# Layer 0's output projection by Strassen's seven products of quarters, in a two-layer retention and attention backbone

## The chip, the cores and the metric

The kernel runs on one core of one Trainium2 chip. The metric is device microseconds for one launch. A core has TensorE (PE in the profile, with its weight loads as PEld), VectorE (DVE), ScalarE (ACT), GpSimd (POOL) and SyncE (SP). Each engine takes its own instructions strictly in order and waits on semaphores; here SP issues all loads, and ACT issues the stores.

## The reference, cut to what matters

Two layers, one of retention and one of windowed attention, are applied to 256 latent tokens; 256 context tokens go through layer 0 with them. The model width is 2048, layer 0 has 8 heads of 512 value features. What the change touches is the end of layer 0, for all 512 tokens:

```python
def finish(o, g):
    b, h, l, dv = o.shape
    on = o * lax.rsqrt(jnp.mean(o * o, axis=-1, keepdims=True) + EPS)
    on = on.transpose(0, 2, 1, 3).reshape(b, l, h * dv) * norm_gain.astype(jnp.float32)
    return (on.astype(g.dtype) * jax.nn.silu(g)) @ w_out
...
x = x + gt_l[:, None] * y_l
if with_ctx_out:
    ctx = ctx + gt_c * y_c
```

So the operand u (4096 features by 512 tokens) is the normalised retention output times a gate, and the output projection is a product of a 2048 x 4096 weight with u. Everything is float32.

## The kernel before, in words

**Precision.** A float32 matrix product is made of three matmuls in a rounded 32-bit format: each operand is split into a high part (ACT casts it, `split`, `split_w`) and a low part (DVE subtracts the high part from the operand, `sub`, line 112). `mm3` adds high times high, high times low and low times high into one PSUM bank, each matmul streaming 512 columns. The kernel has a second form in layer 1 (`gemm_ws2`, lines 166 to 205): high and low part of 256 tokens lie side by side, so that one matmul of 512 columns does high times (high, low), and one of 256 columns does low times high.

**Weights.** Each weight piece is a 512 KB tile of 128 x 1024 (`wraw`, three buffers), loaded by SP, cast by ACT (line 131, `wh`, three buffers) and subtracted on DVE (line 112, `wl`, three buffers). In the three-matmul form one piece feeds 24 matmuls.

**Layer 0.** A loop over 8 heads makes gates, queries and keys, scores, values and outputs. A queue of small tasks (scores, outputs, norms) is drawn from between weight pieces (`hook`, `pump`). Each head's gated output is multiplied by its norm and gain (`spill`) and stored to DRAM in `uT_d`, head by head, because the next head needs the space. While the heads run, DVE also computes the modulation vectors of both layers as dot products (line 632).

**The output projection before.** Four chunks of 512 output features; each takes all 16 pairs of feature blocks of u, 24 matmuls a pair. The first chunk loads and splits u (`u_load`) while head 7's last tasks run in it. The epilogue of a chunk multiplies by the gate vector, adds the residual x, stores the latent half and squares it for the next norm (`residual`, `square`). The last chunk's tail is split by token half, so that the next norm's scale is ready early. Then the attention layer's keys follow (`k_part`), with the modulation of x1 (`mod1`) between weight pieces.

**What sets the order.** A scheduler orders each engine's instructions when the kernel is built, from the order in which the code is written, the data and the buffers' release; on the chip the order is fixed.

## Time and profile before

| what | value |
| --- | --- |
| time, median of 3 runs | 1997.96 us (1997.8 to 1998.27) |
| the profiled execution's own time | 1997.04 us |
| its span, from first to last instruction | 1995.2 us |
| TensorE busy | 1971.2 us, 99% of the span |
| VectorE busy | 1189.7 us, 60% |
| ScalarE busy | 682.3 us, 34% |
| GpSimd busy | 259.2 us, 13%, 89 instructions |
| granted TensorE clock | 1.00 |

The rows of the profile name a line of the kernel, an engine, an operation, what it writes and reads, and the shape as partitions times elements. A matmul's duration in a row covers its whole passage, while matmuls follow each other faster than that; so the pace of TensorE is read from the starting times of a run of them. Idle time in a row belongs to the instruction's engine and is named with what ended it.

### The profile page before, as it was taken

What the parts mean: (1) busy time and instruction counts of PE and PEld (TensorE: products, weight loads), DVE (VectorE), ACT (ScalarE), POOL (GpSimd) and SP (SyncE); (2) the same over time, 40 slices, a digit from 0 to 9 for tenths busy, and PEclk for the clock granted to TensorE, in tenths of its full rate; (3) what the DMA queues carried; (4) which work ended last, traced back from release to release, by engine and by line L of the source; (5) the groups of instructions that cost most, each with busy time, mean ns of one, the idle gap of its engine ahead of it and who ended that gap; (6) DMA issues with size and microseconds to landing.
All of it is one profiled execution on the core that took longest, in us unless ns stands there. A gap on an engine that the chain in (4) does not pass through costs nothing.

```text
span 1995.2 us, 24873 instructions
## 1 busy us (share of the span) xinstructions
PE 1971.2 (99%) x9381; PEld 1626.1 (82%) x9381; DVE 1189.7 (60%) x2320; ACT 682.3 (34%) x1003; POOL 259.2 (13%) x89
## 2 busy tenths in 40 slices
PE   6999999999999999999999999999999999999999
PEld 3678888888888888888888888888888888888887
DVE  5566224778788787786565345433232755777764
ACT  4234223232232232232232234322122434766653
POOL 1217414104104004004000001000000010000001
PEclk9999999999999999999999999999999999999999
DMA  9962334656556555655554335733332234444455
GB/s 377 417 224 87 103 102 147 198 179 201 173 184 187 183 185 179 190 185 179 190 186 166 107 99 165 275 105 108 102 107 95 95 101 156 140 137 130 150 195 170
DMA packets 121080, 332.24 MB, mean 167 GB/s; under 512 B 12480, under 2 KB 27136, under 8 KB 116736
## 3 DMA queue, kind: packets, MB, share of 16 engines
q1 hardware_dynamic: 107312, 315.95, 47.9%
q10 hardware_dynamic: 13648, 14.72, 2.2%
q8 instruction: 73, 1.20, 0.2%
q14 instruction: 47, 0.39, 0.1%
HBM read 318.00 MB, written 12.62 MB: 166 GB/s over the span
## 4 chain that ended last, share of the span: by engine, by line
PE 95%; DMA 2%; DVE 1%; issue 1%; ACT 0%; SPq 0%; POOL 0%; POOLq 0%; DVEq 0%; ACTq 0%
PE acc L138 25%; PE acc L139 25%; PE acc L140 25%; PE acc L189 5%; PE acc L186 3%; PE pm L138 3%; PE pm L140 3%; PE pm L139 3%; PE acc L476 2%; DMA araw<-in_adaS 1%; PE pm L413 1%; PE pm L1048 1%; DMA rows<-gamT_d 1%; DMA xp<-in_xT 0%; PE pm L247 0%
## 5 line engine op out<-in xcount | busy, mean ns | idle before, releaser
L112 DVE TENSOR_TENSOR wl<-wraw,wh 128x1024 fp32r<-128x1024 f32 x368 | 450.0, 1225 | 579.6 <-ACT wh L131 577.9
L131 ACT CAST wh<-wraw 128x1024 fp32r<-128x1024 f32 x367 | 385.0, 1052 | 957.6 <-PE acc L139 582.5
L138 PE MATMUL acc<-hT_h,wh 128*128 128x512 f32 x1184 | 462.8, 391 | 0.6 <-DVE r_l L112 0.6
L139 PE MATMUL acc<-hl,wh 128*128 128x512 f32 x1184 | 461.1, 389 | 0.0
L140 PE MATMUL acc<-hT_h,wl 128*128 128x512 f32 x1184 | 460.7, 389 | 0.0
L632 DVE SCALAR_TENSOR_TENSOR ajunk<-abraw,crow 128x512 bf16<-128x512 f32 x448 | 320.1, 714 | 8.6
L140 PE MATMUL acc<-wh,hl 128*128 128x512 f32 x704 | 274.1, 390 | 0.0
L138 PEld LDWEIGHTS acc<-hT_h,wh 128*128 128x128 f32 x1184 | 222.4, 188 | 46.8 <-issue 1.3
L140 PEld LDWEIGHTS acc<-hT_h,wl 128*128 128x128 f32 x1184 | 222.3, 188 | 46.7
L139 PEld LDWEIGHTS acc<-hl,wh 128*128 128x128 f32 x1184 | 222.5, 188 | 44.3
L693 POOL TENSOR_TENSOR dd<-two,dd 128x128 f32<-128x128 f32 x8 | 167.9, 20995 | 486.4 <-DVE dd L691 486.4
L139 PE MATMUL acc<-wl,hT_h 128*128 128x512 f32 x576 | 224.4, 390 | 0.0
L138 PE MATMUL acc<-wh,hT_h 128*128 128x512 f32 x576 | 224.3, 389 | 0.0
L140 PEld LDWEIGHTS acc<-wh,hl 128*128 128x128 f32 x704 | 132.1, 188 | 28.1 <-DVE hl L273 0.7
L138 PEld LDWEIGHTS acc<-wh,hT_h 128*128 128x128 f32 x576 | 108.2, 188 | 22.2 <-issue 0.3
L139 PEld LDWEIGHTS acc<-wl,hT_h 128*128 128x128 f32 x576 | 108.2, 188 | 21.9
L239 POOL TENSOR_TENSOR rs<-ms,mhalf 128x4 f32<-128x4 f32 (+1 forms) x23 | 32.5, 1412 | 616.8 <-DVE ms L236 324.0
L743 POOL TENSOR_TENSOR ossq<-ossq,osq 128x512 f32<-128x512 f32 x24 | 31.3, 1306 | 414.5 <-ACT osq L740 414.5
L138 PE MATMUL acc<-wh,hl 128*128 128x512 f32 x192 | 75.5, 393 | 0.0
L139 PE MATMUL acc<-wl,hl 128*128 128x512 f32 x192 | 74.8, 390 | 0.0
L138 PE MATMUL pm<-r_h 128*128 128x512 f32 (+1 forms) x208 | 71.5, 344 | 0.0
L140 PE MATMUL pm<-r_h,r_l 128*128 128x512 f32 (+1 forms) x208 | 71.2, 342 | 0.0
(233 smaller groups left out, 2374.3 us busy)
## 6 DMA issues: line engine op xcount, KB each, us to landing
wraw<-in_w SPq DMA_DIRECT2D x272, 512.0 KB, 3.5
abraw<-in_adaB SPq DMA_DIRECT2D x256, 256.0 KB, 3.2
wraw<-in_wo SPq DMA_DIRECT2D x96, 512.0 KB, 3.5
araw<-in_adaS SPq DMA_DIRECT2D x28, 1024.0 KB, 13.0
uT_d<-ue ACTq DMA_DIRECT2D x32, 256.0 KB, 2.8
wraw<-uT_d SPq DMA_DIRECT2D x16, 512.0 KB, 4.2
araw<-in_adaS SPq DMA_DIRECT2D x8, 512.0 KB, 9.4
x<-in_xT SPq DMA_DIRECT2D x4, 1024.0 KB, 8.0
```

The source lines that it names most:

```text
L112: return nc.vector.tensor_tensor(out=out, in0=a, in1=hi.bitcast(F32), op=ALU.subtract)
L131: last_hi[0] = nc.scalar.copy(wh, raw).ins
L138: nc.tensor.matmul(ps, lhsT=ah, rhs=bh, start=start, stop=False, skip_group_check=skip)
L139: nc.tensor.matmul(ps, lhsT=ah, rhs=bl, start=False, stop=False, skip_group_check=skip)
L140: return nc.tensor.matmul(ps, lhsT=al, rhs=bh, start=False, stop=stop, skip_group_check=skip).ins
L186: nc.tensor.matmul(accs[j][:, 0:L], lhsT=wk, rhs=h1(kb, s)[:, 0], start=False, stop=(kb == 2 * nkp - 1))
L189: nc.tensor.matmul(accs[j], lhsT=wk, rhs=h1(kb, s).rearrange("p a t -> p (a t)"), start=(kb == 0), stop=False)
L239: nc.gpsimd.tensor_tensor(out=rs, in0=ms, in1=mhalf.to_broadcast([P, n]), op=ALU.pow)
L476: last = nc.tensor.matmul(qk0[j], lhsT=a_[:, kb % 2, j * P:(j + 1) * P], rhs=b_, start=(kb == 0 and p == 0), stop=(kb == KB - 1 and p == 2))
L632: nc.vector.scalar_tensor_tensor(out=junk, in0=raw, scalar=1.0, in1=crow[:, t, q * 512:(q + 1) * 512], op0=ALU.mult, op1=ALU.mult, accum_o ...
L693: nc.gpsimd.tensor_tensor(out=dd, in0=two.to_broadcast([P, P]), in1=dd, op=ALU.pow)
L743: nc.gpsimd.tensor_tensor(out=ssq, in0=ssq, in1=sq, op=ALU.add)
```

## The change

The product is computed by Strassen's scheme over quarters. The 4096 features of u are split in two halves (in each head the first and the last two blocks of 128), the tokens in latent and context, the output features in two halves of 1024. Seven products M1 to M7, each of a 1024 x 2048 weight combination with a 2048 x 256 operand combination, replace eight.

- **Operands.** `parts` makes the five sums and differences of u's quarters that five products need, and stores them with the two plain quarters in `uB_d`; on GpSimd for heads 0 to 6, and for head 7 on DVE where the first two products need them. `prep` loads such a piece, and `split` makes its high and low part, side by side.
- **Weights.** `quarter` loads one 512 KB tile of a quarter of the weight, `comb` adds or subtracts two of them on GpSimd (128 x 1024), and `split_w` follows as before. M4 and M3 take a plain quarter, the other five a combination. The tiles come from a ring of seven buffers (three as before, four that held the low part of the layer's input).
- **Matmuls.** `piece` is the second form above: 8 matmuls of 512 columns and 8 of 256 for one weight tile. Four rounds r of 256 output features, in each four steps kq, and two products at a time: stage 1 is M4 with M1, stage 2 M5 with M7, stage 3 M2 with M6, stage 4 M3 alone.
- **Epilogue.** `done1` to `done4` add and subtract the products into x1 (ACT copies one half of a bank, DVE adds the other, GpSimd joins products with `comb`); `residual` now loads x piece by piece. The latent half is complete after stage 3, so its modulation runs under stage 4 (`hook4`).
- **Last head.** Head 7's gate product moves to the end of the layer, with the output tasks and the first operand loads between its weight pieces; its gating comes after it.

The host's layout of the weight changes to match. In the middle of the projection the engines' orders differ as follows.

**GpSimd, in the program before, from the end of the heads on.** The rows are the running sum of squares of a head's outputs (`ossq`), a reciprocal root (`rs`), the two reciprocal roots behind the projection (128x2), and then at once the attention layer's tables.

```order
L743 TENSOR_TENSOR ossq_9675<-ossq_9675,osq_9740 128x512
L743 TENSOR_TENSOR ossq_9675<-ossq_9675,osq_9793 128x512
L743 TENSOR_TENSOR ossq_9675<-ossq_9675,osq_9846 128x512
L239 TENSOR_TENSOR rs_9893<-ms_9891,mhalf_86 128x4
L239 TENSOR_TENSOR rs_11867<-ms_11864,mhalf_86 128x2
L239 TENSOR_TENSOR rs_11942<-ms_11939,mhalf_86 128x2
...
L949 TENSOR_TENSOR ktab_12298<-ropeA_12293,vec_72 128x128
```

Between the fourth and the fifth of these rows GpSimd had nothing to do for the whole projection.

**GpSimd, in the change, around the second round of stage 3.** `wraw` are tiles of the weight ring, combined by `comb` (line 911); `tmp` is M2 on its way into x1.

```order
L911 TENSOR_TENSOR wraw_11846<-wraw_11844,wraw_11846 128x1024
L911 TENSOR_TENSOR wraw_11848<-wraw_11844,wraw_11848 128x1024
L911 TENSOR_TENSOR x1_9874<-x1_9874,tmp_9877 128x2x256
L911 TENSOR_TENSOR wraw_11894<-wraw_11892,wraw_11894 128x1024
L911 TENSOR_TENSOR wraw_11896<-wraw_11892,wraw_11896 128x1024
L911 TENSOR_TENSOR wraw_11948<-wraw_11946,wraw_11948 128x1024
L911 TENSOR_TENSOR wraw_11950<-wraw_11946,wraw_11950 128x1024
L911 TENSOR_TENSOR wraw_12010<-wraw_12008,wraw_12010 128x1024
L911 TENSOR_TENSOR wraw_12012<-wraw_12008,wraw_12012 128x1024
L911 TENSOR_TENSOR wraw_12072<-wraw_12070,wraw_12072 128x1024
L911 TENSOR_TENSOR x1_9874<-x1_9874,tmp_9877 128x2x256
```

Now every weight tile of stages 2 and 3 passes through GpSimd first, two a step, and the join of a finished product stands between them in the same queue.

**VectorE, in the program before, at the end of a chunk.** `wl` is the low part of a weight piece, L846 the residual out of PSUM (`acc`), L859 the sum of squares.

```order
L112 TENSOR_TENSOR wl<-wraw,wh 128x1024 x15
L846 SCALAR_TENSOR_TENSOR x_10312<-acc,gt_91,x_10312 128x256 x4
L859 TENSOR_TENSOR ssq_10313<-ssq_10313,pm 128x512
L846 SCALAR_TENSOR_TENSOR x_10312<-acc,gt_91,x_10312 128x256
L859 TENSOR_TENSOR ssq_10313<-ssq_10313,pm 128x512
L846 SCALAR_TENSOR_TENSOR x_10312<-acc,gt_91,x_10312 128x256 x3
L112 TENSOR_TENSOR wl<-wraw,wh 128x1024
L859 TENSOR_TENSOR ssq_10313<-ssq_10313,pm 128x512 x2
```

Sixteen subtractions to a chunk, with the epilogue after them.

**VectorE, in the change, at the end of a round of stage 3.** L937 adds the two halves of M2's banks, L1032 subtracts M2 from x1, L941 adds M6 out of its banks, L960 is the residual out of a loaded x tile.

```order
L960 SCALAR_TENSOR_TENSOR x1_9874<-x1_9874,gt0_91,wraw_12220 128x256 x2
L112 TENSOR_TENSOR wl_12242<-wraw_12236,wh_12241 128x1024
L112 TENSOR_TENSOR wl_12269<-wraw_12238,wh_12268 128x1024
L937 TENSOR_TENSOR tmp_9877<-acc_12066,tmp_9877 128x256
L937 TENSOR_TENSOR tmp_9877<-acc_12067,tmp_9877 128x256
L1032 TENSOR_TENSOR x1_9874<-x1_9874,tmp_9877 128x2x256
L112 TENSOR_TENSOR wl_12304<-wraw_12298,wh_12303 128x1024
L941 TENSOR_TENSOR x1_9874<-acc_12068,x1_9874 128x256
L941 TENSOR_TENSOR x1_9874<-acc_12069,x1_9874 128x256
...
L112 TENSOR_TENSOR wl_12325<-wraw_12300,wh_12324 128x1024
```

Eight subtractions to a round, 28 rounds of a product instead of four chunks, and an epilogue between them that also waits for the round's matmuls.

```diff
+    uB_d = dram.tile([7, H, P, 2, L], F32, name="uB_d")
...
+    home = {M4: R_[0:8], M1: R_[8:10] + T_[0:5] + H_[7:8], M5: h_, M7: H_[5:7] + R_[2:8],
+            M2: R_[0:2] + R_[8:10] + T_[0:4], M6: T_[4:5] + H_[7:8] + R_[2:8], M3: h_}
...
+    ring, ring_n = [None] * 3, [0]
+
+    def raw_tile():
+        i = ring[ring_n[0] % len(ring)]
...
+    def prep(m, us):
+
+        raw = raw_tile().rearrange("p h (f t) -> p h f t", f=2)
+        nc.sync.dma_start(out=raw[:, :len(us)], in_=uB_d[m, us[0]:us[-1] + 1].rearrange("h p f t -> p h f t"))
+        for i, u in enumerate(us):
+            b = unit(m, u)
+            split(b[:, :, 0:L], b[:, :, L:T], raw[:, i])
...
+            if gated:
+                nc.vector.tensor_tensor(out=sg[:, f, :], in0=op, in1=sg[:, f, :], op=ALU.mult)
+            else:
+                nc.scalar.copy(sg[:, f, :], op)
...
+        def parts(h, u, to=None):
+
+            a, b, c, d = (u[:, 2 * k:2 * k + 2, L * t:L * t + L] for k in range(2) for t in range(2))
+            for m, x, y, op in ((M4, a, c, ALU.subtract), (M1, a, d, ALU.add), (M6, a, b, ALU.add),
+                                (M7, c, d, ALU.add), (M3, b, d, ALU.subtract)):
+                ue = pb.tile([P, 2, L], F32, name="ue", tag="ue", bufs=2)
+                now = to is not None and m in (M1, M4)
+                (nc.vector if now else nc.gpsimd).tensor_tensor(out=ue, in0=x, in1=y, op=op)
+                if now:
+                    split(to[m][:, :, 0:L], to[m][:, :, L:T], ue)
+                else:
+                    nc.scalar.dma_start(out=uB_d[m, h], in_=ue)
+            for m, x in ((M2, a), (M5, d)):
+                nc.scalar.dma_start(out=uB_d[m, h], in_=x)
...
+        sg = pb.tile([P, 4, 512], F32, name="sg", tag="sg")
+        output_tasks(H - 1, sg, gated=False)
+        for i, u in zip((1, 2, 4, 5, 7), range(2, 7)):
+            tasks.insert(i, lambda u=u: prep(M1, [u]))
+        for u in range(7):
+            tasks.append(lambda u=u: prep(M4, [u]))
+            if u < 2:
+                tasks.append(lambda u=u: prep(M1, [u]))
+        accs = gemm_ws(w0_d, 3 * H - 1, 8, h_mov, T, hook=lambda: pump(3), tail=2)
+        for f in range(4):
+            z = pb.tile([P, T], F32, name="z", tag="pt", bufs=2)
+            nc.scalar.activation(z, accs[f], AF.Silu)
+            nc.vector.tensor_tensor(out=sg[:, f, :], in0=sg[:, f, :], in1=z, op=ALU.mult)
+        while tasks:
+            pump()
+        parts(H - 1, sg, {m: unit(m, H - 1) for m in (M1, M4)})
...
-    accs0 = gemm_ws(wo0_d, 0, 16, u_slot, T, pre=last_head)
+    ring[:] = [None, H_[0], None, H_[1], None, H_[2], H_[3]]
...
+        def comb(out, a, b, op):
+            nc.gpsimd.tensor_tensor(out=out, in0=a, in1=b, op=op)
+            return out
+
+        def piece(accs, w, m, kq):
+
+            wh, wl = (x.rearrange("p a (k c) -> p (a k) c", k=2) for x in w)
+            for js in ([[0, 1]] if kq < 3 else [[0], [1]]):
+                for lo in range(2):
+                    for j in js:
+                        for k in range(4):
+                            b = unit(m, 2 * kq + k // 2)[:, k % 2, :]
+                            wk = (wl if lo else wh)[:, k, j * P:(j + 1) * P]
+                            if lo:
+                                nc.tensor.matmul(accs[j][:, 0:L], lhsT=wk, rhs=b[:, 0:L], start=False,
+                                                 stop=(kq == 3 and k == 3))
+                            else:
+                                nc.tensor.matmul(accs[j], lhsT=wk, rhs=b, start=(kq == 0 and k == 0), stop=False)
...
+                nc.scalar.copy(out, acc[:, L:T])
+                nc.vector.tensor_tensor(out=out, in0=acc[:, 0:L], in1=out, op=ALU.add)
+
+        def added(out, acc):
+            for c in (lat, cx):
+                nc.vector.tensor_tensor(out=out, in0=acc[:, c], in1=out, op=ALU.add)
...
+        def stage(ms, weights, done, hook):
+            for r in range(4):
+                accs = {m: [acc_tile() for _ in range(2)] for m in ms}
+                n1, n2 = slice(2 * r, 2 * r + 2), slice(8 + 2 * r, 10 + 2 * r)
+                for kq in range(4):
+                    for m, w in zip(ms, weights(r, kq)):
+                        piece(accs[m], w, m, kq)
+                        if kq == 3:
+                            done(r, m, accs[m], n1, n2)
+                    hook(r, kq)
+
+        def weights1(r, kq):
+            b, a = quarter(1, 1, r, kq), quarter(0, 0, r, kq)
+            yield split_w(b)
+            yield split_w(comb(a, a, b, ALU.add))
...
+        def weights2(r, kq):
+            a, b, c = quarter(0, 0, r, kq), quarter(0, 1, r, kq), quarter(1, 1, r, kq)
+            yield split_w(comb(a, a, b, ALU.add))
+            yield split_w(comb(c, b, c, ALU.subtract))
+
+        def done2(r, m, accs, n1, n2):
+            if m == M5:
+                for j in range(2):
+                    merged(x1[:, 2 * r + j, cx], accs[j])
+            else:
+                for j in range(2):
+                    added(x1[:, 2 * r + j, lat], accs[j])
+                comb(x1[:, n1, lat], x1[:, n1, lat], x1[:, n1, cx], ALU.subtract)
+
+        def hook2(r, kq):
+            if r and kq == 2:
+                residual([2 * r - 2, 2 * r - 1])
+            if kq == 1:
+                prep(M2, [2 * r, 2 * r + 1])
+            if (r, kq) == (2, 2):
+                prep(M6, [0, 1])
+            if (r, kq) == (0, 0):
+                prep(M7, [6, 7])
+            if r == 3 and kq > 1:
+                prep(M6, [2 * kq - 2, 2 * kq - 1])
...
+        def weights3(r, kq):
+            a, b, c = quarter(1, 0, r, kq), quarter(1, 1, r, kq), quarter(0, 0, r, kq)
+            yield split_w(comb(b, a, b, ALU.add))
+            yield split_w(comb(c, a, c, ALU.subtract))
+
+        def done3(r, m, accs, n1, n2):
+            if m == M2:
+                t = tmp[:, r % 2]
+                for j in range(2):
+                    merged(t[:, j], accs[j])
+                comb(x1[:, n2, lat], x1[:, n2, lat], t, ALU.add)
+                nc.vector.tensor_tensor(out=x1[:, n2, cx], in0=x1[:, n2, cx], in1=t, op=ALU.subtract)
+            else:
+                for j in range(2):
+                    added(x1[:, 8 + 2 * r + j, cx], accs[j])
+
+        def hook3(r, kq):
+            if (r, kq) == (0, 0):
+                prep(M6, [6, 7])
+            if kq == 2:
+                residual([2 * r + 6, 2 * r + 7])
+            if kq == 1:
+                prep(M3, [2 * r, 2 * r + 1])
+
+        stage((M4, M1), weights1, done1, hook1)
+        stage((M5, M7), weights2, done2, hook2)
+        stage((M2, M6), weights3, done3, hook3)
...
+        def weights4(r, kq):
+            yield split_w(quarter(0, 0, r, kq))
+
+        def done4(r, m, accs, n1, n2):
+            t = tmp4[:, r % 2]
+            for j in range(2):
+                merged(t[:, j], accs[j])
+                for kb in (2 * r + j, 8 + 2 * r + j):
+                    nc.vector.scalar_tensor_tensor(out=x1[:, kb, cx], in0=t[:, j], scalar=gt0[:, kb, 1:2],
+                                                   in1=x1[:, kb, cx], op0=ALU.mult, op1=ALU.add)
+                    square(kb, cx)
...
+            for kb in range(16 * n // 12, 16 * (n + 1) // 12):
+                if kb % 2 == 0:
+                    hl[kb // 2] = r1.tile([P, 2, T], F32R, name="hl", tag=f"hl{kb // 2}")
+                with tc.issue_after(last_hi[0]), tc.issue_after(last_lo[0]):
+                    nc.scalar.activation(x1[:, kb, lat], x1[:, kb, lat], AF.Copy, scale=gs1[:, kb, 0:1])
+                    comb(x1[:, kb, lat], x1[:, kb, lat], rB[:, lat], ALU.mult)
+                    modulate1(kb, 0)
...
+        for kp in range(3):
             w[kp] = load_w(w1_d[0, kp])
+            k_part(kp, (0, 1))
+        for kp in range(8):
+            if kp >= 3:
+                w[kp] = load_w(w1_d[0, kp])
             for kb in (2 * kp, 2 * kp + 1):
-                for s in range(2):
-                    mod1(kb, s, rB)
-            k_part(kp, range(4))
+                mod1(kb, bp if kb < 2 else rB)
+            if kp == 0:
+                nc.scalar.copy(rB[:, cx], bp[:, cx])
```

More of the change, by code (lines that the diff above doesn't have):

```diff
@@ L642, in ada_jobs @@
             close_top()
-            open_slots("r2y")
+            open_top("wx")
         jobs = ada_jobs()
@@ L773, in last @@
                     spill(h, f + i, sg, st["bp"])
-            for f in range(4):
-                tasks.append(lambda f=f: first(f))
+                if f and gated:
+                    parts(h, sg)
+            for f in (0, 2):
+                tasks.append(lambda f=f: (first(f), first(f + 1)))
             tasks.append(norm)
```

164 lines of the change are left out of this document (85 added, 79 removed).

## The prediction

> **What bounds the kernel now.** I read the page's busy shares and its chain of waits first, then the groups of instructions, and then stretches of the projection.
>
> ```profile
> span 1995.2 us, 24873 instructions
> PE 1971.2 (99%) x9381; PEld 1626.1 (82%) x9381; DVE 1189.7 (60%) x2320; ACT 682.3 (34%) x1003; POOL 259.2 (13%) x89
> PE 95%; DMA 2%; DVE 1%; issue 1%; ACT 0%; SPq 0%; POOL 0%; POOLq 0%; DVEq 0%; ACTq 0%
> ...
> L112 DVE TENSOR_TENSOR wl<-wraw,wh 128x1024 fp32r<-128x1024 f32 x368 | 450.0, 1225 | 579.6 <-ACT wh L131 577.9
> L131 ACT CAST wh<-wraw 128x1024 fp32r<-128x1024 f32 x367 | 385.0, 1052 | 957.6 <-PE acc L139 582.5
> ```
>
> TensorE carries 95% of the chain. The weight split waits for it, not the other way round: VectorE stood idle 577.9 us behind ScalarE's cast, and ScalarE 582.5 us behind the matmul that frees a buffer.
>
> ```profile
> core 0: us, PE busy (x) PEld busy (x) DVE busy (x) ACT busy (x) POOL busy (x), PEclk, DMA share, GB/s
> 20.00:45.00 25.00, 23.84 (x144) 13.99 (x144) 12.06 (x39) 7.86 (x15) 1.01 (x1) 1.00 1.04 401
> 1180.00:1290.00 110.00, 110.00 (x509) 91.89 (x508) 55.50 (x73) 41.81 (x62) 5.83 (x4) 1.00 0.60 205
> 1290.00:1370.00 80.00, 80.00 (x354) 66.24 (x354) 23.30 (x26) 17.52 (x19) 0.00 (x0) 1.00 0.34 110
> ```
>
> Inside the projection (the last two rows) TensorE has no gap and its granted clock is 1.00, VectorE works 23.30 of 80 us and GpSimd not at all. So here a matmul taken out is worth its whole pace, there is no bubble to win, and whatever the new work costs beyond TensorE's own time is a loss.
>
> **Matmuls: minus 35 us.** The pace, from starts of the three-matmul form and of the paired form:
>
> ```profile
> 1299.80 0.39 PE L139 MATMUL acc<-r_l,wh 128*128 128x512 f32 x1
> ...
> 1307.05 0.39 PE L138 MATMUL acc<-r2y_h,wh 128*128 128x512 f32 x1
> ...
> 1912.46 2.00 PE L189 MATMUL acc<-hT_h,wh 128*128 128x512 f32 x8
> 1914.30 1.12 PE L186 MATMUL acc<-hT_h,wl 128*128 128x256 f32 x8
> 1915.26 2.00 PE L189 MATMUL acc<-hT_h,wh 128*128 128x512 f32 x8
> ```
>
> 32 starts in 7.25 us are 0.2266 us a matmul. The projection has 4 x 16 x 24 = 1536 of them (48 as two halves): 348.1 us. A new piece, 8 of 512 columns and 8 of 256, takes 1915.26 - 1912.46 = 2.80 us; seven products of 16 pieces are 112 x 2.80 = 313.6 us. Difference -34.5, call it -35. All other matmuls stay, head 7's gates included.
>
> **Weight combinations: plus 76 us.** Each of the 64 pieces of stages 2 and 3 needs one GpSimd sum of 128x1024 (`comb`), one cast and one VectorE subtraction. Alone each would fit. But the rows show that a GpSimd sum and a VectorE operation with two operands in SBUF don't run together:
>
> ```profile
> L112 DVE TENSOR_TENSOR hl<-wraw,hT_h x16: 684/691/1816, 1201.4 to 1249.3; 128x512 fp32r<-128x512 f32 x16
> ...
> 1232.62 1.81 DVE L112 TENSOR_TENSOR hl<-wraw,hT_h 128x512 fp32r<-128x512 f32 x1
> ...
> 1232.60 1.29 POOL L743 TENSOR_TENSOR ossq<-ossq,osq 128x512 f32<-128x512 f32 x1 [6.02 <-ACT osq L740]
> ...
> 1087.77 0.69 DVE L741 TENSOR_TENSOR sg<-pm,sg 128x512 f32<-128x512 f32 x1
> 1088.38 1.33 DVE L632 SCALAR_TENSOR_TENSOR ajunk<-abraw,crow 128x512 bf16<-128x512 f32 x1
> ...
> 1087.88 1.29 POOL L743 TENSOR_TENSOR ossq<-ossq,osq 128x512 f32<-128x512 f32 x1 [6.25 <-ACT osq L740]
> ...
> 1224.14 1.29 DVE L112 TENSOR_TENSOR hl<-wraw,hT_h 128x512 fp32r<-128x512 f32 x2
> ...
> 1225.26 1.32 POOL L743 TENSOR_TENSOR ossq<-ossq,osq 128x512 f32<-128x512 f32 x1 [122.15 <-ACT osq L740]
> ...
> L743 POOL TENSOR_TENSOR ossq<-ossq,osq x24: 1287/1287/1662, 255.8 to 1241.9; 128x512 f32<-128x512 f32 x24
> L1100 POOL TENSOR_TENSOR xo<-xo,half 128x256 f32<-128x256 f32 x12 | 8.6, 737 | 93.9 <-DVE xo L1098 93.9
> ```
>
> The subtraction of 0.69 us took 1.81 under a sum and ended at 1234.43, 0.54 after the sum's end (1233.89); the dot product at 1088.38 also ended 0.54 after its sum (1089.71 against 1089.17). The multiplication ahead of it, with one operand in PSUM, kept its 0.69. The other way round, the sum at 1225.26 ended 1.15 us after VectorE's (1225.43). So one waits for the other's whole data phase: 0.54 us for 512 elements on VectorE, 1.15 on GpSimd, only the start-up hidden. From 256 to 512 elements GpSimd's time grows by 1.287 - 0.737 = 0.55 us; by that an estimate for 1024 is 2.39 us alone and 1.15 + 1.10 = 2.25 held. VectorE's piece is 1.225 alone and 2 x 0.54 = 1.07 held (rounded).
>
> Held time, stage by stage, against TensorE's 32 x 2.80 = 89.6 us:
> - Stage 1: 16 combinations x 2.25 + 32 subtractions x 1.07 = 70.2; 14 operand units to split, 7.6; four joins of 128x512, 4.6; three sums for head 7, 3.5. Sum 85.9: just under.
> - Stage 2: 32 x (2.25 + 1.07) = 106.2; 16 units, 8.6; 12 residuals of 256 elements at 0.27, 3.2; joins 4.6. Sum 122.6.
> - Stage 3: 106.2; 10 units, 5.4; 16 residuals, 4.3; joins 4.6; four differences on VectorE, 2.2. Sum 122.7.
>
> Stages 2 and 3 lose 245.3 - 179.2 = 66 us if the pair never rests. It rests a little at each round's end: the order puts two additions out of PSUM ahead of GpSimd's join, which waits for them, and nothing then holds the operands. I take 1.2 us (two additions of 0.41, row below, and the way between queues) for each of eight rounds: 66 + 10 = 76. With no start-up hidden the sums are 137.7 and 138.3 (2.39 and 1.225 a piece, 0.69 a unit, 0.48 a residual, 1.29 a join), a loss of 97. For stage 1, at 96% of TensorE's time and with waits for PSUM between, I take 3 (0 to 8).
>
> ```profile
> L693 POOL TENSOR_TENSOR dd<-two,dd 128x128 f32<-128x128 f32 x1 | 21.1, 21109 | 93.4 <-DVE dd L691 93.4
> ...
> L112 DVE TENSOR_TENSOR wl<-wraw,wh 128x1024 fp32r<-128x1024 f32 x4 | 4.9, 1221 | 0.4 <-ACT wh L131 0.4
> ```
>
> These two rows, of the 21 us under one GpSimd power, say the opposite: four subtractions kept 1221 ns. The Trainium skill (page "SBUF — State Buffer", section "Who interferes with whom") states that a VectorE instruction with two SBUF inputs and any GpSimd instruction that reads SBUF shut each other out for the whole instruction; by it the sums above hold and the powers should have held too, which they did not, so the measurement decides and the rule is too wide here. The same skill (page "GPSIMD Engine Reference", section "3.1 Elementwise — side-by-side cycle accounting") gives 4497 ns for a sum of 2048 elements; half of it is an estimate of 2.25 us for a combination where mine is 2.39, and by it the loss would be some 9 us smaller (64 x 0.14).
>
> **Stage 4 and the way to the keys: plus 6 and plus 3.** `hook4` puts the latent modulation under the last product.
>
> ```profile
> L273 DVE SCALAR_TENSOR_TENSOR hl<-x,sh,hl 128x256 fp32r<-128x256 f32 x16 | 7.7, 488 | 0.2 <-ACT hl L272 0.2
> L846 DVE SCALAR_TENSOR_TENSOR x<-acc,gt,x 128x256 f32<-128x256 f32 x29 | 12.7, 478 | 3.2 <-PE acc L140 3.2
> L859 DVE TENSOR_TENSOR ssq<-ssq,pm 128x256 f32<-128x256 f32 x3 | 1.2, 414 | 0.0
> ```
>
> VectorE's own time: 16 x 1.225 + 16 x 0.49 + four rounds of 6 x 0.41 + 4 x 0.48 (17.5) = 44.9 us, against TensorE's 16 x 2.80 = 44.8. On top come 16 GpSimd products (0.74 alone), each of which can hold it up by 0.6: 0 to 10. Most of the work lies in the last three rounds; I take 6 (0 to 12). Before, this modulation ran under the keys and cost nothing, and there VectorE now has less to do. The start of stage 1 and the step to the context half's scale get 3 (0 to 8): ScalarE's queue holds stores that wait for GpSimd's sums, with casts behind them, but three cast pieces stand ready.
>
> **At nothing.** Heads 0 to 6 get 35 GpSimd sums of 1.15 held, at most 40 us of VectorE's time; the 577.9 us that it waits for the cast cover them, and without that cover the 40 would be due. The gates of the next head need their space free from these sums; should they come late by 3 us, six heads lose 18. Loads: three tiles in a step of 7.7 us are 1.5 MB, 205 GB/s, which the row of 1180 shows at a share of 0.60. ScalarE has some 3 us in that step (two casts of 1.05, the rest copies).
>
> **Sum.** -35 + 76 + 3 + 6 + 3 = +53 us. The profiled execution's own time is 1997.0; so 2050, and the median of the runs lies 0.9 above: 2051. With all low ends: -35 + 66 = +31, 2029. With all high ends: -35 + 97 + 8 + 12 + 8 = +90, 2088.
>
> **Rivals.**
> - *Faster: the sums don't hold VectorE through.* A combination of 1024 elements may let it in, as the powers do. Then GpSimd needs 32 x 2.39 + 4 x 1.29 = 81.6 us a stage, under 89.6, and the time is 1998 - 35 + some 6 = 1969. For it: the power's rows. Against: the sums of the same kind, and the longest of 1662 ns, which was itself held up. Chance 0.08.
> - *No change.* If combination and subtraction overlap by half of what they hold, so that the three losses make 35: 1998. Chance 0.03.
> - *Slower still: one piece after another.* Combination, cast, subtraction and matmul share in-order queues, and at a round's end VectorE's next subtractions stand behind additions that wait for TensorE. If no lookahead is left, a piece costs 2.39 + 1.05 + 1.225 = 4.67 us, 64 of them 299 us: -35 + 120 + 12 = +97, 2095. It decides from the point where fewer than two pieces are ahead. For it: three `wh` buffers. Against: seven ring tiles, and an order in which the next subtraction stands ahead of those additions. Chance 0.13.
>
> **How the numbers follow.** The forecast, VectorE and GpSimd taking turns as the bound of stages 2 and 3, has 0.76 and gives 2051, its own range 2029 to 2088. The range for all cases goes to 2012 below (a partial overlap) and 2096 above (the third rival). Within 0.2% is about what the runs can tell from no change: faster 0.08, same 0.03, slower 0.89.
>
> **What would show it.** Right: stages 1 and 4 near 92 and 51 us, stages 2 and 3 near 128 each, with TensorE 70% busy there and its idle time ended by ScalarE's `wh` or VectorE's `wl`; the combinations' mean above 2.39 us and the mean of `wl` above 1.225 in these stages, the two together near 3.6 or more; TensorE's starts in a piece still 2.80 apart. Wrong: `wl` at 1.22 under a running combination (first rival), or long stretches in which GpSimd and VectorE both stand idle (third). A stall in the heads or a longer stage 1 would mean that I costed the operand sums or the moved gates too low.

## The result, and the profile after

The change made the kernel slower: 2060.9 us, median of four runs (2058.98 to 2063.59), against 1997.88 us; the ratio is 1.0316, interval 1.0298 to 1.0334. The forecast was 2051 us, with a range of its own of 2029 to 2088. The profiled execution took 2060.75 us, 63.7 more than the profiled one of before.

The page of the changed kernel, its busy shares and three of its groups of instructions:

```profile
span 2059.0 us, 26306 instructions
...
PE 1969.8 (96%) x9589; PEld 1622.3 (79%) x9589; DVE 1447.7 (70%) x2481; ACT 764.6 (37%) x1147; POOL 603.0 (29%) x235
...
L112 DVE TENSOR_TENSOR wl<-wraw,wh 128x1024 fp32r<-128x1024 f32 x416 | 596.6, 1439 | 372.6 <-ACT wh L131 368.5
L131 ACT CAST wh<-wraw 128x1024 fp32r<-128x1024 f32 x415 | 433.6, 1050 | 893.7 <-PE acc L139 311.5
...
L911 POOL TENSOR_TENSOR wraw<-wraw 128x1024 f32<-128x1024 f32 x80 | 237.0, 2984 | 91.2 <-DMA wraw<-in_wo 75.3
```

VectorE's subtraction went from 1225 to 1439 ns in the mean over the whole program, and a combination takes GpSimd 2984 ns. TensorE's busy time hardly fell, mainly because some of its matmuls ran slower (below): the same matmuls take 1940.4 us busy when the sums are left out (first experiment). The four stages in the view of busy time by stretch (each stretch runs from the start of the first matmul of one stage to that of the next):

```profile
core 0: us, PE busy (x) PEld busy (x) DVE busy (x) ACT busy (x) POOL busy (x), PEclk, DMA share, GB/s
1222.00:1316.00 94.00, 90.66 (x513) 78.40 (x512) 76.36 (x63) 46.71 (x64) 54.60 (x21) 1.00 0.64 216
1316.00:1442.00 126.00, 100.53 (x512) 81.00 (x510) 114.80 (x85) 44.48 (x60) 104.11 (x36) 0.96 0.73 250
1442.00:1581.00 139.00, 107.84 (x512) 86.18 (x511) 120.73 (x98) 44.87 (x59) 98.83 (x36) 0.88 0.65 218
1582.00:1630.00 48.00, 46.13 (x265) 39.74 (x264) 42.66 (x72) 35.60 (x69) 16.90 (x17) 1.00 0.49 165
```

In stages 2 and 3 VectorE is shown as busy for 91 and 87% of the time and GpSimd for 83 and 71%, since an instruction that waits for the other engine counts as busy. What they wait for shows in the durations over these two stages (shortest, median and longest, in ns):

```profile
L112 DVE TENSOR_TENSOR wl<-wraw,wh x64: 1208/2315/3422, 1315.5 to 1577.7; 128x1024 fp32r<-128x1024 f32 x64
...
L911 POOL TENSOR_TENSOR wraw<-wraw x62: 2365/3344/3762, 1318.2 to 1571.0; 128x1024 f32<-128x1024 f32 x62
```

A combination alone takes 2.365 us and a subtraction 1.208; in the median they take 3.34 and 2.32. So the combination is held for about VectorE's whole data phase (0.98 us against 1.07), and the subtraction in the median for half of GpSimd's 2.25, at the longest (3.42) for all of it. The estimate from the rows of before was 2.39 alone; half of the figure of the Trainium skill (page "GPSIMD Engine Reference", section "3.1 Elementwise — side-by-side cycle accounting"), 2.25, an estimate, is below the shortest one here.

| stage | TensorE's own time | forecast | changed kernel | no sums | sums on VectorE | sums made, not used |
| --- | --- | --- | --- | --- | --- | --- |
| 1 (M4, M1) | 89.6 | 92.6 | 94.0 | 89.5 | 94.2 | 93.7 |
| 2 (M5, M7) | 89.6 | 127.4 | 126.3 | 89.5 | 107.8 | 125.0 |
| 3 (M2, M6) | 89.6 | 127.5 | 139.4 | 89.5 | 104.1 | 134.9 |
| 4 (M3) | 44.8 | 50.8 | 48.6 | 50.1 | 51.9 | 48.7 |

(Microseconds, from the starts of the first matmuls; stage 4 up to the end of its last matmul. The forecast column is the held time plus 4.8 for four rounds' ends in stages 2 and 3; the last three columns are experiments.)

### The profile page after: what moved, and what is told of

It is laid out like the page before. It is cut to its first block, busy times and chain, and to the rows that moved or that the text cites. A ratio compares the mean times of both kernels' runs of the same rounds, so it can differ in the third digit from the quotient of the medians.

```text
span 2059.0 us, 26306 instructions
## 1 busy us (share of the span) xinstructions
PE 1969.8 (96%) x9589; PEld 1622.3 (79%) x9589; DVE 1447.7 (70%) x2481; ACT 764.6 (37%) x1147; POOL 603.0 (29%) x235
## 3 DMA queue, kind: packets, MB, share of 16 engines
q1 hardware_dynamic: 122512, 363.66, 53.5%
## 5 line engine op out<-in xcount | busy, mean ns | idle before, releaser
L112 DVE TENSOR_TENSOR wl<-wraw,wh 128x1024 fp32r<-128x1024 f32 x416 | 596.6, 1439 | 372.6 <-ACT wh L131 368.5
L131 ACT CAST wh<-wraw 128x1024 fp32r<-128x1024 f32 x415 | 433.6, 1050 | 893.7 <-PE acc L139 311.5
L138 PE MATMUL acc<-hT_h,wh 128*128 128x512 f32 x928 | 363.6, 392 | 0.9 <-DVE r_l L112 0.9
L140 PE MATMUL acc<-hT_h,wl 128*128 128x512 f32 x928 | 362.0, 390 | 0.0
L139 PE MATMUL acc<-hl,wh 128*128 128x512 f32 x928 | 361.8, 390 | 0.0
L911 POOL TENSOR_TENSOR wraw<-wraw 128x1024 f32<-128x1024 f32 x80 | 237.0, 2984 | 91.2 <-DMA wraw<-in_wo 75.3
L138 PEld LDWEIGHTS acc<-hT_h,wh 128*128 128x128 f32 x928 | 174.7, 188 | 37.8 <-DVE r_l L112 1.3
L140 PEld LDWEIGHTS acc<-hT_h,wl 128*128 128x128 f32 x928 | 174.7, 188 | 36.7
L139 PEld LDWEIGHTS acc<-hl,wh 128*128 128x128 f32 x928 | 174.7, 188 | 35.0
L803 POOL TENSOR_TENSOR ue<-sg 128x512 f32<-128x512 f32 x38 | 66.5, 1766 | 73.8 <-DVE sg L793 46.3
L927 PE MATMUL acc<-bop,wh 128*128 128x512 f32 x224 | 65.8, 432 | 19.1 <-ACT wh L131 11.9
```

The costliest lines, as they stand in the source:

```text
L112: return nc.vector.tensor_tensor(out=out, in0=a, in1=hi.bitcast(F32), op=ALU.subtract)
L131: last_hi[0] = nc.scalar.copy(wh, raw).ins
L138: nc.tensor.matmul(ps, lhsT=ah, rhs=bh, start=start, stop=False, skip_group_check=skip)
L139: nc.tensor.matmul(ps, lhsT=ah, rhs=bl, start=False, stop=False, skip_group_check=skip)
L140: return nc.tensor.matmul(ps, lhsT=al, rhs=bh, start=False, stop=stop, skip_group_check=skip).ins
L803: (nc.vector if now else nc.gpsimd).tensor_tensor(out=ue, in0=x, in1=y, op=op)
```

## The experiments

Where no range is given, the time is that of a single run.

**The sums left out.** Does the stall come from the sums at all, or from three loaded tiles a step?

```diff
         def weights2(r, kq):
             a, b, c = quarter(0, 0, r, kq), quarter(0, 1, r, kq), quarter(1, 1, r, kq)
-            yield split_w(comb(a, a, b, ALU.add))
-            yield split_w(comb(c, b, c, ALU.subtract))
+            yield split_w(a)
+            yield split_w(c)
```

> The changed kernel without the weight sums of stages 1 to 3: every tile is loaded as before, but a plain quarter is split where a combination was, so the five products use other weights and the output is not the reference's. Theory A (GpSimd's sum and VectorE's two-operand work take turns): nothing holds the subtractions any more, `wl` goes back to about 1.23 us, stages 2 and 3 are TensorE's, 90 to 95 us each instead of 126 and 138; about 2061 - 35 - 45 = 1980 us. Rival B (late loads: three tiles a step, and GpSimd idle behind loads for some 64 us in stages 1 to 3): the loads are the same, stages 2 and 3 stay above 110; above 2010 us.

Measured: 1971.3 us. Stages 1 to 3 take 89.5 us each, TensorE without a gap (the second line covers most of stage 2 and the start of stage 3):

```profile
L112 DVE TENSOR_TENSOR wl<-wraw,wh x64: 1211/1224/2328, 1313.3 to 1489.7; 128x1024 fp32r<-128x1024 f32 x64
...
1316.00:1420.00 104.00, 104.00 (x598) 91.42 (x597) 76.60 (x102) 52.01 (x69) 6.44 (x4) 1.00 0.95 350
```

The same tiles are loaded at a transfer share of 0.95 and 350 GB/s, and TensorE waits for nothing. So rival B (late loads) falls: the loads can keep up. That GpSimd's idle time behind loads in the changed kernel came from buffers that were freed late fits this, but is not shown by itself. The run also prices the rest of the change: 1971.3 is 8 us above 1997.9 - 34.5, of which stage 4 has 5.3.

**The sums made, but not used.** Is it the exclusion itself, or the chain from sum to cast to subtraction to matmul?

```diff
-            yield split_w(comb(a, a, b, ALU.add))
-            yield split_w(comb(c, b, c, ALU.subtract))
+            comb(b, a, b, ALU.add)
+            yield split_w(a)
+            comb(b, b, c, ALU.subtract)
+            yield split_w(c)
```

> In stages 2 and 3 GpSimd makes a sum of the same size from the same tiles as in the changed kernel, but the matmuls take a plain quarter, so no cast waits for GpSimd (other weights in four products: the output is not the reference's). Theory A (the exclusion itself costs the time): VectorE is held as before, `wl` stays near 2.3 us in stages 2 and 3, these stay at 115 to 128 us each; 2040 to 2060 us. Rival C (the chain of sum, cast, subtraction and matmul in in-order queues): with the sum out of the chain the stages fall below 100 each; below 2000 us.

Measured: 2053.5 us, stages 2 and 3 at 125.0 and 134.9 us. Durations in these stages:

```profile
L112 DVE TENSOR_TENSOR wl<-wraw,wh x65: 1207/2242/3431, 1315.2 to 1574.4; 128x1024 fp32r<-128x1024 f32 x65
...
L911 POOL TENSOR_TENSOR wraw<-wraw x62: 2385/3242/3411, 1317.8 to 1563.5; 128x1024 f32<-128x1024 f32 x62
```

No cast waits for a sum any more, and yet the kernel gains only 7 us. The chain (rival C) explains about those; the rest is there as soon as both engines work, whether the sums are used or not.

**A PSUM operand.** Is it the second operand in SBUF that VectorE waits with?

```diff
+        if z is not None:
+            for a in range(2):
+                last_lo[0] = nc.vector.tensor_tensor(out=wl[:, a], in0=raw[:, a], in1=z, op=ALU.subtract).ins
+            return wh, wl
...
-            yield split_w(comb(a, a, b, ALU.add))
+            yield split_w(comb(a, a, b, ALU.add), z0)
```

> The changed kernel, with GpSimd's sums as they are, but in stages 2 and 3 the subtraction that makes `wl` takes its second operand from a PSUM bank of zeros instead of `wh`: two operations of 128x512, about 0.69 us each, 1.38 for a piece where it was 1.23 (the low parts are then the whole weights and the output is not the reference's; to make room one bank fewer serves the small products). Theory A in its narrow form (only an operation with two operands in SBUF is shut out by a GpSimd sum): these operations keep 0.69 us under a running sum, the sums go back to about 2.39, and what is left to exclude are units, residuals and joins: 32 x 2.39 + 8.6 + 3.2 + 4.6 = 93 us in stage 2 and about 95 in stage 3; 95 to 105 us each with waits, 2061 - 28 - 36 = about 1997 us. If every VectorE operation that reads SBUF is shut out: stages of 126 to 145 us, 2055 us or more.

Measured: 2020.0 us; stage 2 took 102.6 us, stage 3 120.0. Durations there:

```profile
L135 DVE TENSOR_TENSOR wl<-wraw,z x126: 670/678/692, 1314.8 to 1531.8; 128x512 fp32r<-128x512 f32 x126
...
L916 POOL TENSOR_TENSOR wraw<-wraw x62: 2364/2412/2927, 1317.1 to 1526.0; 128x1024 f32<-128x1024 f32 x62
...
L113 DVE TENSOR_TENSOR hT_h<-wraw,hT_h x8: 1257/2424/2900, 1428.9 to 1518.1; 128x512 fp32r<-128x512 f32 x8
```

Of 126 subtractions with a PSUM operand none took longer than 692 ns, while GpSimd's 62 sums ran at 2412 ns in the median; the operand units, with both operands in SBUF, still took 2424 where they need 0.69 alone. This is the exclusion in its narrow form, as the Trainium skill states it for VectorE's side (page "SBUF — State Buffer", section "Who interferes with whom": one dedicated and one shared read port). Since this subtraction doesn't wait for the cast either, a small part of the gain may be the shorter chain. The time came out 23 us above the expected 1997: stage 3 stayed 25 us above my 95, though the weight subtractions no longer collide.

**What makes stage 3 longer than stage 2.** Three attempts. First, ScalarE's queue stood 27 us before squares that wait for residuals, with casts behind:

```diff
-                nc.scalar.dma_start(out=x1_d[kb], in_=x1[:, kb, lat])
-                square(kb, lat)
+        def settle(kbs):
+            for kb in kbs:
+                nc.scalar.dma_start(out=x1_d[kb], in_=x1[:, kb, lat])
+                square(kb, lat)
```

> The store and the square of a latent residual are issued one step later than the residual, so that ScalarE's queue no longer stands before them (it stood 27 us behind the residual in stage 3 and 5 us in stage 2, with casts of weights behind it). If these waits are what makes stage 3 some 10 us longer than the held times add up to: stage 3 about 128, stage 2 about 124, 2048 us. If they are only time that the exclusion would take anyway: 2061 us, within 3.

Measured: 2059.97 us (2058.67 to 2064.15), stage 3 137.2 us. There is no gain that can be told, but the run doesn't test the theory, for the wait is still there. The view of waits for stage 3 (engine and line, what it waited for, us in total, times, longest), first of the changed kernel, then of this run:

```profile
ACT pm L950 <- DVE x L960: 27.1, 8, 8.0
...
ACT pm L950 <- DVE x L960: 25.0, 8, 5.9
```

The scheduler put the stores and squares between the same casts again; the edit changed the code's order, not ScalarE's in stage 3. So this theory stays open.

Second, GpSimd's join. The end of a round of stage 3 in the changed kernel, in order of time (the bracket is the engine's idle time ahead and what ended it):

```profile
1534.28 4.77 DVE L960 SCALAR_TENSOR_TENSOR x<-x,gt,wraw 128x256 f32<-128x256 f32 x2
...
1536.96 0.39 ACT L950 ACTIVATE pm<-x 128x256 f32<-128x256 f32 x1 [3.68 <-DVE x L960]
1537.29 1.03 ACT L131 CAST wh<-wraw 128x1024 fp32r<-128x1024 f32 x1
...
1538.37 2.07 PE L927 MATMUL acc<-bop,wh 128*128 128x512 f32 x4 [2.21 <-ACT wh L131]
...
1543.42 1.91 PE L927 MATMUL acc<-bop,wh 128*128 128x512 f32 x4
...
1546.22 0.37 ACT L936 COPY tmp<-acc 128x256 f32<-128x256 f32 x1 [2.19 <-PE acc L924]
...
1546.63 0.42 DVE L937 TENSOR_TENSOR tmp<-acc,tmp 128x256 f32<-128x256 f32 x1 [2.14 <-ACT tmp L936]
...
1547.13 1.79 POOL L911 TENSOR_TENSOR x<-x,tmp 128x512 f32<-128x512 f32 x1 [5.87 <-DVE tmp L937]
...
1548.53 1.08 PE L927 MATMUL acc<-r_l,wh 128*128 128x512 f32 x4
1548.89 3.38 POOL L911 TENSOR_TENSOR wraw<-wraw 128x1024 f32<-128x1024 f32 x1
```

The first four lines are the first theory's chain: two residuals took 4.77 us (0.48 each alone), the square waited for them, the cast stood behind the square, and TensorE idled 2.21 us before that cast. Then GpSimd stood 5.87 us before the join of M2, which waits for the additions out of M2's bank, and the next round's combinations are queued behind it.

```diff
-                comb(x1[:, n2, lat], x1[:, n2, lat], t, ALU.add)
+                nc.vector.tensor_tensor(out=x1[:, n2, lat], in0=x1[:, n2, lat], in1=t, op=ALU.add)
```

> The join of M2 into the latent half of x1 (128x512, four times in stage 3) on VectorE instead of GpSimd. In stage 3 GpSimd stood 17.4 us before this join, 5.8 each time, behind `tmp`, with the next step's sums queued behind the join; in stage 2 the join cost 2.2. Theory D (that wait is what makes stage 3 some 10 us longer than the held times): stage 3 falls from 139 to about 128, 2050 us. Rival (the rounds' ends are slow for another reason, and the wait only shows it): 2058 to 2062 us.

Measured: 2055.7 us (2052.43 to 2057.0), ratio to the kernel before 1.0289 (1.0272 to 1.0306), against 1.0316 (1.0298 to 1.0334); stage 3 134.2 us. About half of what theory D expected: 5 us, which the two intervals, overlapping a little, put near the limit of what can be told. The wait before the join is gone, but GpSimd now waits elsewhere in the stage (view of waits):

```profile
POOL wraw L911 <- DVE wl L112: 19.8, 4, 6.0
ACT tmp L936 <- PE acc L924: 19.1, 8, 3.2
POOL wraw L911 <- DMA wraw<-in_wo: 18.7, 15, 2.2
```

Third, the slow clock. Where TensorE idles, its granted clock drops to 0.50; four matmuls at 1538.37 took 2.07 us, four at 1548.53 1.08.

```diff
+                    if lo == 0 and m in (M2, M6):
+                        junk = m_tile()
+                        for k in range(2 * len(js)):
+                            nc.tensor.matmul(junk, lhsT=wh[:, k, 0:P], rhs=unit(m, 2 * kq + k // 2)[:, k % 2, :],
+                                             start=True, stop=True)
```

> In stage 3 four further matmuls a piece (512 columns, into a bank that nobody reads) are issued between the high and the low part: 32 x 4 x 0.2266 = 29 us of work for TensorE, which idles some 45 us there. Theory E (the granted clock, 0.5 to 0.83 in several stretches of 10 us of stage 3, is lost because TensorE idles, and the slow pieces at the rounds' ends hold up VectorE and GpSimd): the clock of stage 3 rises to 0.95 or more, stage 3 becomes shorter by 4 to 10 us, 2051 to 2057 us. Rival (the low clock is only a symptom): stage 3 stays at 139 or grows by a few us, 2060 to 2075 us.

Measured: 2070.2 us (2069.09 to 2070.7); stage 3 147.5 us:

```profile
1441.00:1588.00 147.00, 128.63 (x638) 107.26 (x637) 105.08 (x98) 42.76 (x58) 89.53 (x35) 0.92 0.63 219
```

The clock rose only from 0.88 to 0.92, and the stage became 8 us longer. The filler didn't give what E needs, a clock above 0.95, so E is not excluded; but filling TensorE's idle time in this way is no remedy.

**Other ways to make the sums.** All on VectorE:

```diff
+        def combv(out, a, b, op):
+            nc.vector.tensor_tensor(out=out, in0=a, in1=b, op=op)
+            return out
...
-            yield split_w(comb(a, a, b, ALU.add))
-            yield split_w(comb(c, b, c, ALU.subtract))
+            yield split_w(combv(a, a, b, ALU.add))
+            yield split_w(combv(c, b, c, ALU.subtract))
```

> The weight sums of stages 1 to 3 on VectorE instead of GpSimd, nothing else. Theory A: a sum costs VectorE 1.23 us where on GpSimd it held it up for about 2.25, so VectorE's own work bounds stages 2 and 3. Stage 2: 64 x 1.225 + 16 units of 0.69 + 12 residuals of 0.48 + 20 additions of 0.41 + four joins of 1.15 = 108; stage 3 about 113; with some 5 us of waits at the rounds' ends 113 and 118 instead of 126 and 138, stage 1 below 92. About 2061 - 13 - 20 - 1 = 2027 us. If GpSimd and VectorE in truth worked side by side and the stall came from somewhere else, moving 98 us of sums (80 x 1.225) to VectorE would lengthen the stages: 2070 us or more.

Measured: 2010.7 us, 50 below the changed kernel, though VectorE does 98 us more work of its own. In stages 2 and 3 it is the bound (the first window ends 2.8 us before stage 2 does, the second begins 1.8 us before stage 3):

```profile
1316.00:1420.00 104.00, 93.64 (x497) 78.06 (x496) 95.97 (x116) 44.30 (x59) 20.71 (x4) 0.97 0.86 291
1421.00:1526.00 105.00, 95.21 (x514) 80.61 (x514) 102.63 (x124) 45.49 (x59) 8.74 (x4) 0.98 0.86 295
```

Stage 3 lost its excess over stage 2 (104.1 against 107.8). The expected 2027 was too high by 16: stages 2 and 3 took 5 and 14 us less than the 113 and 118 expected. Stage 3 took even less than the 113 that the expectation had put down for VectorE's own work, so not only the waits at the rounds' ends but also that sum was too high. Stage 1, expected below 92, stayed at 94.2.

By the transfers, for M5 and M2:

```diff
+        def quarter2(n1, k1, n2, k2, r, kq):
+            t = quarter(n1, k1, r, kq)
+            nc.gpsimd.dma_start(out=t.rearrange("p a t -> p (a t)"),
+                                in_=wo0_d[n2, k2, r, kq].rearrange("p k c -> p (k c)"), accum_op=ALU.add)
+            return t
```

> In stages 2 and 3 the sums of M5 and M2 are made by the transfers: a tile is loaded and the second quarter is loaded onto it with addition (128 x 1024, issued by GpSimd, one tile more a step); the differences of M7 and M6 go to VectorE. Theory A: VectorE keeps 48 operations of 1.23 us a stage (59) + 16 units (11) + residuals and additions (14) + joins 4 = 88, below TensorE's 89.6, and GpSimd has no sum left that would hold it; stages 2 and 3 about 92 each, 2061 - 34 - 47 = 1980 us. If an added load is slow or GpSimd's issuing of it holds VectorE as a sum does (no run here has shown such a transfer yet): stages of 110 and more, 2015 us or above.

Measured: 2068.4 us (2063.0 to 2070.39), stages 2 and 3 132.9 and 136.1 us. The page's queues and issues, and the two stages:

```profile
q1 hardware_dynamic: 122512, 363.66, 52.1%
q0 software_dynamic: 4608, 16.78, 4.5%
...
wraw<-in_wo SPq DMA_DIRECT2D x176, 512.0 KB, 5.2
...
wraw<-in_wo POOLq DMA_DIRECT2D x32, 512.0 KB, 8.0
...
1314.00:1446.00 132.00, 102.19 (x507) 87.01 (x506) 82.34 (x102) 43.33 (x60) 19.47 (x19) 0.87 0.98 296
1447.00:1582.00 135.00, 101.90 (x507) 86.30 (x506) 86.34 (x111) 43.49 (x59) 22.59 (x20) 0.90 0.94 285
```

VectorE has time to spare (82 of 132 us busy) and the transfers are the bound, at a share of 0.98: the adding ones take 4.5% of the span for 16.78 MB, plain ones 52.1% for 363.66 MB, so 1.9 times as long a byte, and a tile lands 8.0 us after its issue. The stall has only changed its place.

**A version that beats both?** If VectorE bounds stages 2 and 3, what it adds in the epilogue counts in full. With 24 matmuls of 256 columns a piece, the products of high and low parts fall into one half of a bank, and the addition of two halves is not needed:

```diff
+                            if m in three:
+                                for c in ((lat, cx) if not lo else (lat,)):
+                                    nc.tensor.matmul(accs[j][:, 0:L], lhsT=wk, rhs=b[:, c],
+                                                     start=(kq == 0 and k == 0 and not lo and c is lat),
+                                                     stop=(kq == 3 and k == 3 and lo == 1))
...
-            for c in (lat, cx):
-                nc.vector.tensor_tensor(out=out, in0=acc[:, c], in1=out, op=ALU.add)
+            nc.vector.tensor_tensor(out=out, in0=acc[:, lat], in1=out, op=ALU.add)
```

> The kernel with the weight sums on VectorE, and of the further changes only the 24 matmuls of 256 columns a piece in stages 2 and 3. Theory A says that VectorE is the bound there, so 16 additions of 0.41 us less a stage shorten each by 6.6: 2010.7 - 13 = 1998 us, stages 2 and 3 near 99. If TensorE were the bound, the stages would be longer by 32 x 0.04 = 1.3 us each: 2013 us.

Measured: 1993.4 us, where 1998 was expected. Stages 1 to 3 (the windows set the boundary of 2 and 3 2.4 us early; from the first matmuls the two took 102.3 and 97.5 us):

```profile
1220.00:1311.50 91.50, 90.53 (x513) 78.41 (x513) 74.09 (x77) 46.07 (x64) 10.32 (x6) 1.00 0.69 225
1311.50:1411.50 100.00, 93.44 (x754) 90.91 (x753) 92.19 (x102) 43.13 (x58) 12.84 (x4) 1.00 0.88 302
1411.50:1511.40 99.90, 96.20 (x784) 94.63 (x785) 97.41 (x113) 46.81 (x63) 13.83 (x5) 1.00 0.91 322
```

More matmuls, and stages shorter by 5.5 and 6.6 us, where 6.6 was expected of VectorE's bound and 1.3 more of TensorE's: it was VectorE's. The granted clock rose as well, from 0.97 and 0.98 to 1.00, so a part of the gain may be TensorE's. The same kernel again, timed repeatedly:

> The kernel with the weight sums on VectorE and 24 matmuls of 256 columns a piece in stages 2 and 3, unchanged, timed in rounds against the kernel before: 1993 us, 0.2% below it, if the one look was typical.

Measured: 1995.9 us (1991.66 to 1998.14, eleven runs), ratio 0.9989, interval 0.998 to 0.9998: a hair below the kernel before, inside the 0.2% that counted as no change.

Two attempts to get further. With the residual's product on ScalarE, x added by a transfer, the joins on VectorE and the new form in stage 4:

```diff
+        def residual_dma(kbs):
+            for kb in kbs:
+                for s in range(2):
+                    c = (lat, cx)[s]
+                    nc.scalar.activation(x1[:, kb, c], x1[:, kb, c], AF.Copy, scale=gt0[:, kb, s:s + 1])
+            nc.gpsimd.dma_start(out=x1[:, kbs[0]:kbs[-1] + 1, :], in_=xT_d[:, kbs[0]:kbs[-1] + 1, :], accum_op=ALU.add)
```

> An attempt at a version below both kernels, by theory A: all weight sums and the joins of stages 2 and 3 on VectorE, and VectorE relieved of what others can do. (a) In stages 2 to 4 a piece is 24 matmuls of 256 columns (high times high, high times low, low times high into the same 256 columns) instead of 8 of 512 and 8 of 256: at the 0.118 us at which such matmuls follow each other in the scores, 2.84 us a piece instead of 2.80, and each product then needs no addition of two halves. (b) For six of eight pairs of feature blocks the residual's product with the gate goes to ScalarE and x is added by a transfer. VectorE then has 78 of sums and subtractions + 11 units + 3 + 3 = 95 us in stage 2 and 99 in stage 3 against TensorE's 91, where the kernel with only the sums moved took 105.7 and 106.3; stage 4 two less. 2010.7 - 17 - 2 = 1992 us. If the adding transfers (256 KB each, six) or ScalarE's longer queue hold up the casts, 2000 us or more.

Measured: 2022.8 us (2019.17 to 2023.32), stages 2 and 3 about 110 us each. Its waits in stages 2 to 4:

```profile
ACT wh L131 <- DVE wraw L915: 45.3, 23, 5.3
...
ACT pm L962 <- DMA x<-in_xT: 17.3, 3, 6.3
...
PE acc L931 <- ACT wh L131: 16.8, 7, 6.9
```

ScalarE's queue stands up to 6.3 us behind a landing transfer, with casts behind it. Without the residual's part:

```diff
-                comb(x1[:, n1, lat], x1[:, n1, lat], x1[:, n1, cx], ALU.subtract)
+                combv(x1[:, n1, lat], x1[:, n1, lat], x1[:, n1, cx], ALU.subtract)
...
+        three = (M5, M7, M2, M6, M3)
```

> The kernel of 1993.4 us (weight sums on VectorE, 24 matmuls of 256 columns a piece in stages 2 and 3) with two more steps: the eight joins of 128x512 of stages 2 and 3 on VectorE (0.69 us of its own instead of 1.15 held), and the 24-matmul form in stage 4 too, where eight additions of 0.42 fall away for 16 x 0.04 us of TensorE. Theory A (VectorE is still the bound in stages 2 and 3, about 100 us each against TensorE's 91): 8 x 0.46 = 3.7 and some 2 us less, 1988 us. If other waits than VectorE's own work set these stages (its queue standing behind the joins' operands, loads at 0.9 of the transfers' time): 1992 to 1996 us.

Measured: 1997.0 us (1992.85 to 1999.07), ratio 0.9995 (0.9986 to 1.0004), no different from the one without these steps, where 1988 was expected, or 1992 to 1996 by the other theory. At 100 us a stage VectorE's own work is no longer the only bound; which wait has taken its place is not shown. So the residual's part is what cost the other attempt some 26 us.

## Why the prediction was right, and where it was off

The sum against the profiled difference of 63.7 us:

| term | forecast | measured | from |
| --- | --- | --- | --- |
| matmuls | -35 | -34.5 | stages 1 to 3 of 89.5 us without the sums, as 32 x 2.80 |
| stage 1 | +3 | +4.4 | 94.0 - 89.6 |
| stages 2 and 3 | +76 | +86.5 | 36.7 and 49.8 |
| stage 4 | +6 | +3.8 | 48.6 - 44.8 |
| start, keys, heads | +3 | +3.5 | the rest: 63.7 + 34.5 - 4.4 - 86.5 - 3.8 |

- *What bounds the kernel.* Right: before, a matmul taken out was worth its whole pace. Without the sums the kernel gives 1971 us, where the faster rival had 1969.
- *Sum and subtraction take turns.* Right, and shown from three sides: without the sums the stall is gone (89.5), with unused sums it stays (125.0 and 134.9), with a PSUM operand on VectorE the weights' subtractions no longer take part in it (678 ns). In stage 2 the price holds to 1 us: 126.3 against 122.6 + 4.8.
- *Stage 3.* Mis-sized, 139.4 against 127.5. The step that failed is the rest at the rounds' ends, for which I took 1.2 us a round in both stages. In stage 2 GpSimd's join waits for the second product of the step, in stage 3 for M2, the first, and so stands 5.9 us ahead of combinations that others need; moving it won back about 5 us. Where the other 6 to 7 come from stays open: with unused sums the stage still took 134.9, and with the PSUM operand it was 17 us longer than stage 2. Two candidates are left. One is the squares in ScalarE's queue, which wait for residuals that a sum holds up (27.1 us in stage 3, 5.4 in stage 2), with a cast behind them that TensorE needs; no run with the sums on GpSimd took this wait away. The other is the slow clock: 0.88 in this stage, half speed for 34 of its 139 us, so at most 17 us.
- *TensorE's pace.* "Starts in a piece still 2.80 apart" was wrong for many pieces of stages 2 and 3, and TensorE was busy there for 80 and 78% of the time, not 70%, mainly because of the lower clock.
- *At nothing.* The operand sums of heads 0 to 6, the moved gates, the start and the keys together are within 3.5 us, of which the time from the keys' first matmul to the end has 2.6 (428.8 against 426.2); no stall in the heads is left over for them.
- *The rivals.* "Sums don't hold VectorE" is excluded, and loads, which I had put at nothing, are not the bound. "One piece after another" (2095) is not what happens: breaking its chain won 7 us. But at the ends of stage 3's rounds its mechanism, a queue behind an instruction that waits for TensorE, was real.

## What to carry to other kernels

Handing work to an idle engine is free only if the two engines can run side by side: price it in time that each holds what the other needs, here 2.25 + 1.07 us a piece against the 2.80 that the matmuls took, and add it up stage by stage. Where they can't, the slower engine's help can cost more than doing the work oneself: here moving 98 us of sums onto the busier engine made the kernel 50 us faster. And a scheme with fewer multiplications pays only while the additions that it brings fit under the ones that remain; here 35 us of matmuls bought 80 sums, and the best version found stands level with the plain product.

## What the runs showed of the hardware that I had not expected

TensorE's granted clock falls to half after short idle times. From the start of stage 2:

```profile
1329.37 1.55 PE L924 MATMUL acc<-r_h,wl 128*128 128x256 f32 x8 [1.96 <-DVE wl L112]
1330.72 3.26 PE L927 MATMUL acc<-hT_h,wh 128*128 128x512 f32 x8
...
1388.01 2.04 PE L927 MATMUL acc<-hT_h,wh 128*128 128x512 f32 x8
```

Eight matmuls that take 2.04 us took 3.26, soon after an idle time of 1.96 us (only the eight shorter ones of the first row lie between); and between 1472 and 1480 us the clock was 0.50 throughout:

```profile
1472.00:1480.00 8.00, 6.69 (x19) 5.20 (x20) 4.74 (x5) 2.72 (x5) 2.25 (x1) 0.50 0.83 262
```

Half the clock is what the Trainium skill gives for a TensorE that has gone idle (page "TensorE: Matmul & The Clock Gate", section "HAM oscillation — how this bites in real kernels"); it warns of idle times above some 3.4 us. Here one of 1.96 us was followed by it, so the rule is no safe limit for a TensorE that idles again and again. In stages 2 and 3 the trace's record of the granted clock has eight stretches at 0.50, each of 3.41 us or two or three times that, and no idle time of TensorE there was longer than 3.19 us. Without the sums, where TensorE never idles in these stages, there is none. A stall of another engine can thus be paid twice where TensorE's result is awaited next, as at the rounds' ends of stage 3; how much of the stage that is, no run shows.

An addition made by a transfer costs the transfer engines 1.9 times as long a byte as a plain one and lands in 8.0 us instead of 5.2; in a stretch whose plain transfers already take 0.95 of their time at full pace there is no room for it.
